# A transformer block on one core: subtractions and a mask moved from GpSimd to VectorE, and a square-root table issued later

## The chip, the core and the metric

The kernel runs on one core of a Trainium2 chip. The core has engines that work side by side, each through its own list of instructions in order: PE multiplies matrices, DVE, ACT and POOL work on vectors, and SP issues transfers. An instruction waits where its list has come to until what it needs is there, and everything behind it on the same engine waits with it. The metric is the time of one execution on the device, in microseconds (us).

## The reference, cut to what matters

One layer of a diffusion backbone: 512 latent tokens and 256 context tokens of width 1024. Normalization and modulation, one projection of all tokens by `w_in`, four groups of token mixers on its columns, an output projection, and then a mixture of 16 experts. The part in which the change lies:

```python
(na_q, na_k, na_v, dn_qkv, dn_a, dn_b, dn_gate, df_q, df_k, df_v, ft_u) = split_proj(h_lat @ w_in)
...
lower = jnp.where(strict, jnp.einsum('bnhid,bnhjd->bnhij', kb, kc) * decay, 0.0)
t_inv = lax.linalg.triangular_solve(eye + lower, ..., left_side=True, lower=True, unit_diagonal=True)
u = t_inv @ (vc * bc[..., None])
w = t_inv @ (kb * jnp.exp(gc)[..., None])
...
gate, idx = lax.top_k(jnp.swapaxes(aff, 1, 2), cap)
hid = jax.nn.silu(jnp.einsum('becd,edf->becf', xg, w_gate)) * jnp.einsum('becd,edf->becf', xg, w_up)
y = jnp.einsum('becf,efd->becd', hid, w_down) * gate[..., None]
```

The systems `eye + lower` are 64 x 64, one for each chunk, head and direction (two directions, 12 chunks of 64 tokens, 4 heads).

## The kernel before, in words

**The projection.** `w_in` is taken in 22 column blocks of 128. For each, `win` loads the raw weights `wr` by SP, and `win_parts` splits them: ACT copies them into `wh`, a type of lower precision that PE multiplies fast, and POOL makes the low part `wl = raw - wh` (line 255). The input `h` is split alike in `modulate` into `hh` (ACT) and `hl = h - hh`, for even k on DVE and for odd k on POOL (line 339). `proj_ct` then sums three products on PE: wh by hh, wl by hh, wh by hl. `wr`, `wh` and `wl` have two buffers each, so a block's parts are made while PE multiplies the block before, and the next raw load waits for its buffer.

**The order.** A scheduler gives each engine its list. It mixes the column blocks that have no place on the long path (gate, u, the neighbourhood group's q, k, v, the third group's q, k, v) in between the steps of the delta group, whose chain is: five-tap convolution (`acc`, on DVE), transposes, norms (`rs_...`), gates (`gsc`, a chain of small DVE operations that ends in `gg`), decay (`gm`, `bm` by POOL, then DVE), and the triangular systems `LT` (shown in rows as LTQ).

**The triangular systems.** The 16 x 16 blocks on the diagonal of each system are sent through DRAM (`scr`) into `Bt`, one block to a partition, and inverted there by substitution: 15 steps of `tmpb = Bt*TB` and `TB += tmpb` for two directions on DVE. `TB` and `Bt` go back through DRAM (`scr2`) into `TVc`, POOL spreads that into `TV`, and PE multiplies it by `LT`. Only the blocks off the diagonal of LT are wanted in that product. A mask `offd` clears the others; POOL does that after the blocks have been read (lines 603 to 605). `inverse` and `step` then run the recurrence over the chunks. `nql` and `nkl`, which DVE makes, are the low parts of the neighbourhood group's q and k; `dff` belongs to a block of the third group; `oacc` is the delta group's output, which `head_norm` scales.

**After it.** Attention of the other groups and the output projection, whose order on DVE and ACT is pinned, then the experts, whose weights are streamed by SP from the moment the mixers' memory is free. The last expert's output is summed into `XL`, squared on ACT for the final norm, scaled by a reciprocal square root that uses ACT's Sqrt, and stored. Functions of ACT come in tables; a change of table shows as ACT_TABLE_LOAD. One Sqrt of a constant (`small<-iota`) is issued early so that the table is there.

Of the kernel before, what the change touches and what calls it, by code (L numbers as in the profile page):

```python
# [7 lines left out]
F32 = mybir.dt.float32  # L8
I32 = mybir.dt.int32
F32R = mybir.dt.float32r  # L10
AF = mybir.ActivationFunctionType
ALU = mybir.AluOpType
# [27 lines left out]
def bc(ap, shape):  # L40
    return ap.to_broadcast(shape)


def build(tc, I, out):
    nc = tc.nc
    G, SY = nc.gpsimd, nc.sync
# [16 lines left out]
    PE, V, A = (Pinned(e) for e in (nc.tensor, nc.vector, nc.scalar))  # L63
# [3 lines left out]
    def tl(pool, shape, tag, dt=F32):  # L67
        uid[0] += 1
        return pool.tile(shape, dt, name=f"{tag}_{uid[0]}", tag=tag)
# [25 lines left out]
    with contextlib.ExitStack() as es:  # L95
# [18 lines left out]
        def pde():  # L114
            return next(alt)()

        def pb():
            uid[0] += 1
            return ps.tile([128, 1024], F32, name=f"pb_{uid[0]}", tag="pb", bufs=2)

        def load(pool, name, shape, q=None):
            t = tl(pool, shape, name)
            (q or SY).dma_start(t, I[name])
            return t

        def rhalf(c):
            return slice(c * 64, c * 64 + 64)
# [25 lines left out]
        def stg(shape, nm, dt=F32):  # L153

            uid[0] += 1
            return mp.tile(shape, dt, name=f"{nm}_{uid[0]}", tag="mx", bufs=4)
# [11 lines left out]
        def w4(which, shape, nm, dt=F32):  # L168
            uid[0] += 1
            return w4p.tile(shape, dt, name=f"{nm}_{uid[0]}", tag=f"w{which}")  # L170
# [10 lines left out]
        hh = lambda k: hh6[:, k] if k < 6 else hh2[:, k - 6]  # L181
        hl2 = [x12([128, 4, T], "hl", F32R) for _ in range(2)]
        hl = lambda k: hl2[k // 4][:, k % 4]
# [67 lines left out]
        def win_parts(raw):  # L251
            wh = w4("B", list(raw.shape), "wh", F32R)
            wl = w4("C", list(raw.shape), "wl", F32R)
            A.activation(wh, raw, AF.Copy)
            G.tensor_tensor(wl, raw, wh.bitcast(F32), op=ALU.subtract)  # L255
            return wh, wl

        def win(g, m, kh=None):
            return win_parts(win_raw(g, m, kh))
# [13 lines left out]
        with tc.tile_pool(name="st", bufs=1) as st:  # L273
# [3 lines left out]
            hT = tl(st, [128, 8, T], "hT")  # L277
# [53 lines left out]
            def modulate(q):  # L331
                kq = slice(4 * q, 4 * q + 4)
                V.scalar_tensor_tensor(a1[:, kq], mcol[:, 8 + 4 * q:12 + 4 * q, :], 1.0, bc(g1[:, kq].unsqueeze(2), [128, 4, 2]), op0=ALU.add, op1=ALU.mult)
                for k in range(4 * q, 4 * q + 4):
                    for ts, c in ((LAT, 0), (CTX, 1)):
                        A.activation(hh(k)[:, ts], hT[:, k, ts], AF.Identity, bias=mcol[:, k, c:c + 1], scale=a1[:, k, c:c + 1])
                    V.tensor_scalar(hT[:, k, L:T], hT[:, k, L:T], a1[:, k, 0:1], mcol[:, k, 0:1], op0=ALU.mult, op1=ALU.add)
                    V.tensor_scalar(hT[:, k, 0:L], hT[:, k, 0:L], a1[:, k, 1:2], mcol[:, k, 1:2], op0=ALU.mult, op1=ALU.add)
                    (G if k % 2 else V).tensor_tensor(hl(k), hT[:, k], hh(k).bitcast(F32), op=ALU.subtract)  # L339

            def first_half(b):

                w = win_parts(raws[b])
                p = pa() if b < 2 else pb()
                half.append((p[:, 0:512], p[:, 512:768] if b >= 2 else None))
                proj_ct(w, LAT, half[b][0], 0)
                if b >= 2:
                    proj_ct(w, CTX, half[b][1], 0)
# [3 lines left out]
            mod(0)  # L352
            mod(2)
            modulate(0)
            first_half(0)
            mod(1)
            first_half(1)
            m3 = mod(3)
            modulate(1)
            with tc.issue_after(m3):  # L360
                first_half(2)
# [17 lines left out]
        def b4(i, shape, nm, dt=F32):  # L379
            uid[0] += 1  # L380
            return cva.tile(shape, dt, name=f"{nm}_{uid[0]}", tag=f"b4{i}", bufs=1)
# [10 lines left out]
        for b in range(6):  # L392
            w = win(3 + b // 2, b % 2, 1 if b < 4 else None)
            raw = stg([128, NX], "raw")
# [24 lines left out]
        for kk in range(2):  # L419
            for c0, c1 in ((0, 512), (512, T)):  # L420
                for x, ht in enumerate((hh, hl)):
                    for g in range(4):
                        k = kk * 4 + g
# [95 lines left out]
        offd = load(con2, "offd", [128, 2, 64])  # L519
        blkm = load(con2, "blkm", [128, 4])  # L520
        A2 = big("C", "A2", [128, 4, 2, 8, 64])
        LT = LTQ[:, 0:3072].rearrange("p (d n h i) -> p d n h i", d=2, n=6, h=4)
# [42 lines left out]
        for c in range(2):  # L565
            for b in range(4):
                p0 = c * 64 + b * 16
                SY.dma_start(scr[c, :, :, b].rearrange("d u r i -> r (d u) i"),
                             LT[p0:p0 + 16].rearrange("p d n h i -> p (d n h) i")[:, :, b * 16:b * 16 + 16])
        Bt = b4(0, [128, 1024], "Bt")  # L570
        Bk = Bt[0:96, 0:1024].rearrange("p (c d i r) -> p d c i r", d=2, c=2, i=16)
        tmpb = b4(1, [128, 512], "tmpb")[0:96].rearrange("p (d c e) -> p d c e", d=2, c=2)
# [6 lines left out]
        for j in range(15):  # L579

            n, m = 15 - j, j + 1
# [17 lines left out]
        for q in range(2):  # L599
            for c in range(2):  # L600
                SY.dma_start(TVc[rhalf(c), q].rearrange("p d u r -> p (d u) r"), scr2[q, c].rearrange("d u b i r -> (b i) (d u) r"))

        for d in range(2):
            v = LT[:, d].rearrange("p n h i -> p (n h) i")
            G.tensor_tensor(v, v, bc(offd[:, d:d + 1, :], [128, 24, 64]), op=ALU.mult)


        A1t = {}

# [993 lines left out]
        iota = load(sm, "iota", [128, CAP])  # L1603
# [34 lines left out]
        for ee in range(last + 1):  # L1638
            pgt, pup = pb(), pb()
# [18 lines left out]
            if not ee:  # L1658
                hid, hT2 = (w4("B", [128, 1024], nm) for nm in ("hid", "hT2"))
# [3 lines left out]
                OT = w4("C", [128, 512], "OT", F32R)  # L1663
            for n in range(2):
                ns = slice(n * 512, n * 512 + 512)
                A.activation(hid[:, ns], pgt[:, ns], AF.Silu)
                V.tensor_tensor(hid[:, ns], hid[:, ns], pup[:, ns], op=ALU.mult)

            po = pde()
# [8 lines left out]
            for n in range(2):  # L1678
                pt = pa()
                for j in range(4):  # L1680
                    g, k = divmod(4 * n + j, KD)
# [36 lines left out]
            pga, small, share = pde(), w4("C", [128, 3, 4], "small"), tl(sm, [128, 1], "share")  # L1718
# [3 lines left out]
            V.tensor_copy(share, pga[:, 0:1])  # L1722
            gfin = w4("A", [128, D], "gfin")
            SY.dma_start(gfin[0:1], I["gfin"].unsqueeze(0))
            A.activation(small[:, 0, 0:1], iota[:, 0:1], AF.Sqrt)

            def scales(i0, i1):

# [165 lines left out]
```

## Time and profile before

| | |
|---|---|
| median of 3 runs | 1484.89 us (1484.33 to 1486.93) |
| profiled execution | 1486.06 us, span 1484.2 us |
| PE busy | 1329.8 us, 90% of the span |
| DVE busy | 452.4 us, 30% |
| ACT busy | 321.9 us, 22% |
| POOL busy | 237.9 us, 16% |
| mean rate from HBM | 324 GB/s |

The span is what the profile covers, from the first to the last instruction. A row of the profile names an engine, a line of the kernel and an operation as out<-in. DVE, ACT and PE instructions pass through a wrapper, so nearly all of them carry line 59; they are told apart by the tiles they write. Busy time is an average over stages with different limits, so the shares by themselves don't say what a change to one engine is worth.

### The profile page before, as it was taken

The page shows a single profiled execution, that of the slowest core. Times are in us where ns is not written, and L with a number is a line of the kernel's source. Part 1 is how long each engine was busy: PE and PEld are TensorE (multiplying, and loading weights), DVE is VectorE, ACT ScalarE, POOL GpSimd, SP SyncE. Part 2 cuts the span into 40 slices and gives each one's busy share as a digit, 9 for nine tenths or more (in the row PEclk, how much of TensorE's full clock was granted, in tenths as well). Part 3 has the DMA queues.
Part 4 walks back from the last instruction along what each step waited for, and adds up shares of the span by engine and source line. Part 5 has one row for each costly group of instructions (what it writes and reads, how often), then busy time and mean ns, then how long its engine had stood idle before and what let it go on. Part 6 is the DMA issues. An engine that isn't in the chain of part 4 may idle for free.

```text
span 1484.2 us, 20090 instructions
## 1 busy us (share of the span) xinstructions
PE 1329.8 (90%) x8422; PEld 708.6 (48%) x8422; DVE 452.4 (30%) x958; ACT 321.9 (22%) x675; POOL 237.9 (16%) x229
## 2 busy tenths in 40 slices
PE   5998969989899979999899999999999899899886
PEld 3665757776567754343343343343343343243244
DVE  4666643344573560121221211211201201112112
ACT  5424316624575211010010010010010010000113
POOL 2425727532166110000000000000000000000002
PEclk9999989999999989999999999999999999999998
DMA  9341450456684867999999999999999999999995
GB/s 355 118 144 55 107 139 17 144 178 167 231 239 157 340 283 327 427 425 428 426 427 427 427 425 428 426 427 427 427 427 425 429 425 427 427 427 426 427 402 188
DMA packets 86013, 481.56 MB, mean 324 GB/s; under 512 B 31265, under 2 KB 40097, under 8 KB 60834
## 3 DMA queue, kind: packets, MB, share of 16 engines
q1 hardware_dynamic: 85922, 480.27, 81.0%
q8 instruction: 66, 1.08, 0.3%
q14 instruction: 25, 0.20, 0.0%
HBM read 468.84 MB, written 11.40 MB: 324 GB/s over the span
## 4 chain that ended last, share of the span: by engine, by line
PE 61%; DMA 13%; DVE 9%; ACT 4%; issue 3%; POOL 1%; SPq 1%; ACTq 0%; DVEq 0%; POOLq 0%
PE pb L59 33%; PE pa L59 19%; DMA w<-in_wdown 8%; PE pd L59 5%; PE pe L59 5%; DMA w<-in_wup 3%; DMA wm<-in_wmod 2%; ACT A L59 1%; DVE XL L59 1%; DVE RT L59 1%; DVE hid L59 1%; DVE tmpb L59 1%; DVE yhl L59 1%; ACT hid L59 1%; ACT yhl L59 1%
## 5 line engine op out<-in xcount | busy, mean ns | idle before, releaser
L59 PE MATMUL pb<-w,xg 128*64 128x512 f32 x2032 | 458.3, 601 | 2.2 <-DMA w<-in_wup 1.3
L59 PEld LDWEIGHTS pb<-w,xg 128*64 128x64 f32 x2032 | 147.5, 138 | 274.9 <-issue 263.0
L59 PE MATMUL pa<-w,hT 128*64 128x512 f32 (+2 forms) x1152 | 234.4, 550 | 7.6 <-DMA w<-in_wdown 5.6
L1764 POOL TENSOR_TENSOR xo<-XL,gfin 128x384 f32<-128x384 f32 (+1 forms) x12 | 10.5, 909 | 929.7 <-DMA w<-in_wdown 923.7
L59 PEld LDWEIGHTS pa<-w,hT 128*64 128x64 f32 x1152 | 81.9, 138 | 144.8 <-issue 126.9
L59 DVE TENSOR_TENSOR hid<-hid,pb 128x512 f32<-128x512 f32 x32 | 20.6, 684 | 338.0 <-PE pb L59 338.0
L59 PE MATMUL pa<-hh,wh 128*128 128x512 f32 (+1 forms) x240 | 89.9, 388 | 7.1 <-DVE dff L59 4.3
L59 PE MATMUL pa<-hh,wl 128*128 128x512 f32 (+1 forms) x240 | 86.9, 375 | 1.3 <-POOL wl L255 1.3
L59 ACT ACTIVATE hid<-pb 128x512 f32<-128x512 f32 x32 | 17.4, 596 | 271.2 <-PE pb L59 271.2
L59 PEld LDWEIGHTS pb<-OH,xn 128*128 128x128 f32 x512 | 63.5, 200 | 25.1 <-ACT hid L59 12.4
L59 PE MATMUL pb<-OH,xn 128*128 128x128 f32 x512 | 67.7, 290 | 8.2 <-ACT hid L59 7.1
L59 DVE TENSOR_TENSOR hid<-pa,XL 128x512 f32<-128x512 f32 x15 | 10.4, 692 | 208.0 <-PE pa L59 208.0
L59 DVE SCALAR_TENSOR_TENSOR XL<-pe,aff,XL 128x512 f32<-128x512 f32 x60 | 44.8, 747 | 76.2 <-PE pd L59 70.2
L59 PE MATMUL pe<-yhl,OT 64*128 64x512 f32 x120 | 47.4, 458 | 17.7 <-ACT yhl L59 10.2
L255 POOL TENSOR_TENSOR wl<-wr,wh 128x1024 fp32r<-128x1024 f32 (+1 forms) x22 | 50.9, 2315 | 74.6 <-ACT wh L59 71.9
L59 PE MATMUL pd<-yhl,OT 64*128 64x512 f32 x120 | 47.4, 458 | 15.9 <-ACT yhl L59 8.7
L59 DVE SCALAR_TENSOR_TENSOR XL<-pd,aff,XL 128x512 f32<-128x512 f32 x60 | 44.8, 746 | 50.4 <-PE pe L59 46.4
L59 PEld LDWEIGHTS pa<-hh,wh 128*128 128x128 f32 x240 | 47.5, 198 | 23.4 <-issue 5.2
L59 PE MATMUL pa<-hl,wh 128*128 128x512 f32 (+1 forms) x240 | 55.0, 361 | 0.9 <-POOL hl L339 0.9
L59 ACT ACTIVATE yhl<-hid 128x512 fp32r<-128x512 f32 x15 | 9.5, 631 | 203.9 <-DVE hid L59 189.0
L59 PEld LDWEIGHTS pa<-hh,wl 128*128 128x128 f32 x240 | 47.4, 198 | 9.2 <-POOL wl L255 2.3
L59 PEld LDWEIGHTS pa<-hl,wh 128*128 128x128 f32 x240 | 39.6, 188 | 8.6 <-POOL hl L339 1.3
(387 smaller groups left out, 1640.8 us busy)
## 6 DMA issues: line engine op xcount, KB each, us to landing
w<-in_wgate SPq DMA_DIRECT2D x64, 2048.0 KB, 34.0
w<-in_wup SPq DMA_DIRECT2D x63, 2048.0 KB, 35.4
w<-in_wdown SPq DMA_DIRECT2D x60, 2048.0 KB, 35.9
wm<-in_wmod SPq DMA_DIRECT2D x32, 512.0 KB, 7.2
wr<-in_win SPq DMA_DIRECT2D x18, 512.0 KB, 3.4
wm<-in_wmod SPq DMA_DIRECT2D x8, 1024.0 KB, 12.1
w<-in_wdown SPq DMA_DIRECT2D x8, 768.0 KB, 12.6
wr<-in_wout SPq DMA_DIRECT2D x16, 256.0 KB, 5.8
```

The costliest lines, as they stand in the source:

```text
L59: r = f(*args, **kw)
L255: G.tensor_tensor(wl, raw, wh.bitcast(F32), op=ALU.subtract)
L1764: G.tensor_tensor(xo[i][:, cols], xl[:, i, cols], gfin[:, cols], op=ALU.mult)
```

## The change

Three things go from POOL to DVE: the 26 subtractions that make `wl`, the four `hl` of odd k, and the mask on LT. The mask is also written further ahead, in front of the code of the substitution. Fourth, the Sqrt of a constant near the end is issued after the last Silu.

```diff
             A.activation(wh, raw, AF.Copy)
-            G.tensor_tensor(wl, raw, wh.bitcast(F32), op=ALU.subtract)
+            V.tensor_tensor(wl, raw, wh.bitcast(F32), op=ALU.subtract)
             return wh, wl
...
-                    (G if k % 2 else V).tensor_tensor(hl(k), hT[:, k], hh(k).bitcast(F32), op=ALU.subtract)
+                    V.tensor_tensor(hl(k), hT[:, k], hh(k).bitcast(F32), op=ALU.subtract)
...
+        for d in range(2):
+            v = LT[:, d].rearrange("p n h i -> p (n h) i")
+            V.tensor_tensor(v, v, bc(offd[:, d:d + 1, :], [128, 24, 64]), op=ALU.mult)
         Bt = b4(0, [128, 1024], "Bt")
...
-        for d in range(2):
-            v = LT[:, d].rearrange("p n h i -> p (n h) i")
-            G.tensor_tensor(v, v, bc(offd[:, d:d + 1, :], [128, 24, 64]), op=ALU.mult)
...
-                A.activation(hid[:, ns], pgt[:, ns], AF.Silu)
+                silu = A.activation(hid[:, ns], pgt[:, ns], AF.Silu)
...
-            A.activation(small[:, 0, 0:1], iota[:, 0:1], AF.Sqrt)
+            with tc.issue_after(silu.ins):
+                A.activation(small[:, 0, 0:1], iota[:, 0:1], AF.Sqrt)
```

The scheduler then makes new lists, and more moves than the edits say. Three places of the lists follow. The first is DVE's list just ahead of the substitution; the names end in the number of their buffer. Before:

```order
L59 TENSOR_TENSOR nql_2668<-pa_2642,nqh_2667 128x512
L59 SCALAR_TENSOR_TENSOR nkl_2730<-pa_2679,nkh_2729 128x512
L59 SCALAR_TENSOR_TENSOR nkl_2730<-pa_2704,nkh_2729 128x256
L59 TENSOR_SCALAR Bt_1243<-Bt_1243 96x1024
L59 TENSOR_TENSOR tmpb_1244<-Bt_1243,TB_1246 96x2x15 x2
```

The same place on DVE in the changed kernel:

```order
L59 TENSOR_TENSOR wl_2740<-wr_2737,wh_2739 128x1024
L59 SCALAR_TENSOR_TENSOR nkl_2730<-pa_2679,nkh_2729 128x512
L59 SCALAR_TENSOR_TENSOR nkl_2730<-pa_2704,nkh_2729 128x256
L59 TENSOR_TENSOR wl_2803<-wr_2800,wh_2802 128x1024
L59 TENSOR_TENSOR LTQ_876<-LTQ_876,offd_1045 128x1536 x2
L59 TENSOR_TENSOR wl_2860<-wr_2857,wh_2859 128x1024
L59 TENSOR_SCALAR Bt_1245<-Bt_1245 96x1024
L59 TENSOR_TENSOR tmpb_1246<-Bt_1245,TB_1248 96x2x15 x2
```

Three wl and the two halves of the mask now stand ahead of Bt, the first instruction of the substitution; wl_2860, for the second k block of the neighbourhood group, is the last of them.

The second place is DVE's list in `head_norm`, where the copy of a third-group block (dff_3128) stands among the small operations of the norm. Before:

```order
L59 SCALAR_TENSOR_TENSOR rs_z1h_528_3514<-rs_ah_527_3511,rs_z0h_526_3509 128x16
L59 TENSOR_TENSOR rs_ah_529_3516<-rs_z1h_528_3514 128x16
L59 TENSOR_TENSOR rs_ah_529_3516<-rs_ah_529_3516,rs_th_522_3499 128x16
L59 SCALAR_TENSOR_TENSOR rs_z2h_530_3519<-rs_ah_529_3516,rs_z1h_528_3514 128x16
L59 TENSOR_TENSOR oacc_1322<-oacc_1322,rs_z2h_530_3519 128x256
L59 COPY dff_3128<-pa_3103 128x256
```

In the changed kernel:

```order
L59 TENSOR_TENSOR rs_ah_525_3506<-rs_ah_525_3506,rs_th_522_3499 128x16
L59 COPY dff_3128<-pa_3103 128x256
L59 SCALAR_TENSOR_TENSOR rs_z0h_526_3509<-rs_ah_525_3506,rs_jh_524_3503 128x16
L59 TENSOR_TENSOR rs_ah_527_3511<-rs_z0h_526_3509 128x16
L59 TENSOR_TENSOR rs_ah_527_3511<-rs_ah_527_3511,rs_th_522_3499 128x16
L59 TENSOR_TENSOR si_3043<-pa_3135,si_3043 128x512
L59 TENSOR_TENSOR wl_3213<-wr_3210,wh_3212 128x1024
```

The copy is now in front of rs_z0h instead of behind the first oacc.

The third place is the end of ACT's list, from the last expert's one-hot tile (OT) to its hidden units (hid), as a piece of the difference:

```order
+L59 ACTIVATE OT_5443<-pe_8496 128x512
+L59 ACTIVATE hid_5440<-pb_8378 128x512 x2
 L59 ACT_TABLE_LOAD
 L59 ACTIVATE small_8524<-iota_5300 128x1
-L59 ACTIVATE OT_5443<-pe_8496 128x512
-L59 ACT_TABLE_LOAD
-L59 ACTIVATE hid_5440<-pb_8378 128x512 x2
 L59 ACTIVATE gfin_8535<-pe_8578 128x512
```

One table load now stands behind the two Silu, and a later one, behind the last square and ahead of the last small, is gone from the list.

Elsewhere: in the gsc chain of DVE one wl (wl_2605) stands six places ahead of gg, and another behind gg. On POOL the first TV follows directly on operations of the recurrence, where a wl stood ahead of it. On PE the transposes of the convolved keys (pd_881 and on), which begin the chain of norms and gates, stand earlier, ahead of projection matmuls of the gate's second block. On ACT the gate's second Silu stands behind the Exp of the gates instead of ahead of it, with a table load on each side. From the output projection on, the lists of PE and SP and the pinned ones are the same, but for the end.

## Rows read from the trace of the kernel before

**Rows 1.** Windows: each engine's busy time (instructions), PE clock, DMA share, GB/s.

```profile
549.00:1441.00 892.00, 824.53 (x4137) 332.06 (x4137) 142.50 (x220) 71.51 (x129) 0.00 (x0) 0.99 0.99 419
```

**Rows 2.** PE's waits, 40 to 349 us: total us, times, longest.

```profile
PE pa L59 <- DVE nql L59: 9.2, 1, 9.2
PE pe L59 <- DVE gsc L59: 4.8, 1, 4.8
PE pa L59 <- DVE dff L59: 4.3, 1, 4.3
PE pd L59 <- POOL gm L537: 2.3, 3, 0.9
...
PE pb L59 <- POOL TV L619: 1.7, 1, 1.7
...
PE pa L59 <- POOL wl L255: 1.3, 2, 0.8
PE pa L59 <- POOL hl L339: 0.9, 1, 0.9
```

**Rows 3.** Timeline of DVE, 126 to 136 us: start, us, instruction.

```profile
127.97 2.37 DVE L59 TENSOR_TENSOR rs_a<-rs_a,rs_t 128x48 f32<-128x48 f32 x1
...
130.86 0.20 DVE L59 TENSOR_TENSOR rs_a<-rs_a,rs_t 128x48 f32<-128x48 f32 x1
...
134.41 2.38 DVE L59 TENSOR_SCALAR gsc<-gsc 128x48 f32<-128x48 f32 x1
```

**Rows 4.** Timeline of POOL, the same stretch; in brackets the idle time before.

```profile
134.10 2.65 POOL L255 TENSOR_TENSOR wl<-wr,wh 128x1024 fp32r<-128x1024 f32 x1 [3.83 <-ACT wh L59]
```

**Rows 5.** Timeline of DVE, the substitution.

```profile
178.02 1.44 DVE L59 TENSOR_SCALAR Bt<-Bt 96x1024 f32<-96x1024 f32 x1 [5.51 <-DMA Bt<-scr]
179.50 5.71 DVE L59 TENSOR_TENSOR tmpb<-Bt,TB 96x30 f32<-96x30 f32 x2
...
188.54 2.58 DVE L59 TENSOR_TENSOR TB<-TB,tmpb 96x120 f32<-96x120 f32 x2
...
191.52 0.47 DVE L59 TENSOR_TENSOR TB<-TB,tmpb 96x126 f32<-96x126 f32 x2
```

**Rows 6.** Timeline of POOL, from the mask to the first TV.

```profile
175.42 7.40 POOL L605 TENSOR_TENSOR LTQ<-LTQ,offd 128x1536 f32<-128x1536 f32 x2
...
210.04 2.36 POOL L255 TENSOR_TENSOR wl<-wr,wh 128x1024 fp32r<-128x1024 f32 x1 [19.26 <-ACT wh L59]
212.37 2.33 POOL L619 TENSOR_TENSOR TV<-TVc,blkm 128x256 f32<-128x256 f32 x4
```

**Rows 7.** Timelines of DVE and POOL, 301 to 305 us.

```profile
301.62 2.51 DVE L59 TENSOR_TENSOR oacc<-oacc,rs_z2h 128x256 f32<-128x256 f32 x1
304.06 0.41 DVE L59 COPY dff<-pa 128x256 f32<-128x256 f32 x1
...
301.51 2.34 POOL L255 TENSOR_TENSOR wl<-wr,wh 128x1024 fp32r<-128x1024 f32 x1
```

**Rows 8.** POOL's groups by form: xcount, busy us, mean ns, idle before.

```profile
L255 POOL TENSOR_TENSOR wl<-wr,wh 128x1024 fp32r<-128x1024 f32 x18 | 45.2, 2511 | 71.3 <-ACT wh L59 68.7 <-issue 2.6
```

**Rows 9.** DVE's groups by form, 40 to 349 us.

```profile
L59 DVE TENSOR_TENSOR nql<-pa,nqh 128x512 fp32r<-128x512 f32 x2 | 1.4, 682 | 1.1 <-ACT nqh L59 1.1
```

**Rows 10.** Windows, PE alone: length, busy (instructions), granted clock, DMA share, GB/s.

```profile
132.00:138.00 6.00, 6.00 (x49) 0.62 0.37 126
160.00:180.00 20.00, 19.97 (x111) 1.00 0.72 182
304.50:310.50 6.00, 5.98 (x14) 0.50 0.45 109
```

**Rows 11.** Timeline of ACT, after a block of the neighbourhood group.

```profile
181.34 1.09 ACT L59 ACTIVATE wh<-wr 128x1024 fp32r<-128x1024 f32 x1
```

**Rows 12.** Timeline of ACT, the end.

```profile
1445.74 0.60 ACT L59 ACTIVATE gfin<-pe 128x512 f32<-128x512 f32 x1 [4.91 <-PE pe L59]
...
1472.85 1.28 ACT L59 ACT_TABLE_LOAD   x1
1474.14 0.30 ACT L59 ACTIVATE small<-small 128x1 f32<-128x1 f32 x2
```

## The prediction

> **What bounds the kernel now.** I read the 40 slices and the windows first, then PE's waits, then the timelines of DVE, POOL and ACT at those waits, and the end last. From 549 to 1441 us the reader is to see a stage of transfers: 419 GB/s and a DMA share of 0.99, no POOL work at all, little DVE work [rows 1]. Nothing that this change moves can shorten it. But its first loads wait for memory that the mixer stages free, so a front that ends earlier moves the whole of it forward. What matters are the first 349 us and the last 43.
>
> In the front PE runs its list in order, and its waits are few and long [rows 2]: 9.2 us for DVE's nql, 4.8 for DVE's gsc, 4.3 for DVE's dff, 2.3 for POOL's gm, 1.7 for POOL's TV, 1.3 for POOL's wl, 0.9 for POOL's hl. Only the last two are waits for what the change moves. The three longest are for DVE, which gets more work. So the question is why DVE was late there.
>
> **DVE is late because POOL holds it.** Next to each other, the timelines of both engines show it. A 128x48 rs_a takes 0.20 us, but 2.37 when it starts at 127.97; a 128x48 gsc took 2.38 at 134.41 [rows 3]. At 134.10 a wl had begun on POOL, for 2.65 us [rows 4], and the gsc ends when it does (136.8); under the rs_a lies the wl before it. The substitution shows the same: tmpb x2 takes 5.71 us and TB x2 2.58, where a larger TB x2 takes 0.47 [rows 5], and POOL's mask (7.40 us for its two halves, from 175.42) and further wl lie over them [rows 6]. So does the third: oacc 2.51 us, with dff queued behind it, while a wl runs on POOL [rows 7].
> The Trainium skill ("SBUF — State Buffer", Who interferes with whom) says that GpSimd and VectorE share a pair of ports, that a VectorE instruction with two SBUF inputs or in a two-port mode contends with a GpSimd one that reads SBUF, and that the second to issue is blocked until the first is done. The rows agree: the ends coincide. The rule also speaks against the change, since each moved subtraction has two SBUF inputs and can itself be held by what stays on POOL; that is in the first rival.
>
> **The change, part by part.** POOL loses 18 wl of 128x1024 at 2.51 us [rows 8], the smaller wl, four hl and the mask. DVE gets them. Its price isn't shown for 128x1024; a subtraction of 128x512 took 0.68 there [rows 9], so a 1024 is bounded by 0.68 and 1.38, and I take 1.38. DVE is busy for 30% of the span, so the sum is no bound; what counts is where they stand.
>
> First, PE's direct waits before 80 us: 0.9 + 1.3 = 2.2. The same copy on ACT precedes them, and then 1.4 us replaces up to 2.9. DVE is dense there; I take 2.0 (0 to 2.2).
>
> Second, the gsc chain. The two holds go: 2.37 - 0.20 + 2.38 - 0.20 = 4.35. One wl now stands among its last instructions: 1.38. The chain is 3.0 shorter, and of PE's 4.8 us, 1.8 would be left. The transposes that begin the chain also stand ahead of projection matmuls that were ahead of them, which PE can now do while it waits; so I take all 4.8. The clock adds to it. It was 0.62 of full speed in 132 to 138, the 6 us after that gap, in which PE worked without a pause [rows 10]: (1 - 0.62) x 6.0 = 2.3 us. Without the gap that goes too. Together 7.1 (from -1.4, if the inserted wl only adds, to 7.1). POOL's gm (2.3) stays where it is: 0 (0 to 2.3, if POOL starts them sooner).
>
> Third, the substitution. It starts when Bt lands, at 178.02 [rows 5]. It loses holds of (5.71 - 0.47) + (2.58 - 0.47) = 7.3 us. But ahead of it in DVE's list now stands wl_2860. That needs ACT's wh, which in the row of before began at 181.34 for 1.09, behind the copies nvcT and nvT of a projection [rows 11]. On DVE it would end at 181.34 + 1.09 + 1.38 = 183.8, 5.8 us after Bt has landed. PE was busy in all of 160 to 180 [rows 10], so that projection and the triangular systems move forward about alike and the 5.8 stays. Gain: 7.3 - 5.8 = 1.5 (0 to 7.3, if the wait doesn't bind). Queued behind it are the whole substitution and nql, for which PE waits. The mask costs nothing on DVE: it waits only until the transfers out of LT have read it, and Bt's own transfer comes after those; if that cover went, it would be at most the 7.4 of POOL's two.
>
> Fourth, POOL's TV. It is behind a wl at 210.04, itself late on ACT's wh by 19.26 [rows 6]; PE waits 1.7 for it. POOL's list has no wl there now: 1.7 (0 to 1.7).
>
> Fifth, the recurrence to 295. Two or three wl land between its X's on DVE. PE has little idle time there, so I charge 0.5 (0 to 3 x 1.38 = 4.1).
>
> Sixth, the blocks after 295. dff's copy waited behind oacc [rows 7], PE 4.3 us for it. In the new list it stands eight instructions earlier, behind instructions of 0.2 us: perhaps 0.5 is left, gain 3.8. The clock after the gap was 0.50 for 6.0 us [rows 10]: 3.0 more. Together 6.8 (0 to 6.8).
>
> Seventh, the end. ACT loads a table at 1472.85 for 1.28 us, on the path to the output [rows 12]. With the Sqrt issued behind the last Silu, the table is loaded once, in ACT's 4.91 us of idle time before gfin, and stays: 1.3 (0 to 1.3).
> The Trainium skill ("ScalarE: Activation LUTs", What ACT_TABLE_LOAD costs) puts a switch at 1283 ns for the load and 1380 ns more for a drain, 2.66 in all; the trace agrees with the load alone, since small begins 1.29 us after it. By the page this term would be 2.7; the sum goes by the row.
>
> Two more table loads stand in the front of the new ACT list, one ahead of the late gate's Silu and one ahead of eg. I cost them at nothing, as ACT waits there for PE; uncovered they cost 1.28 each.
>
> Sum: 2.0 + 7.1 + 1.5 + 1.7 - 0.5 + 6.8 + 1.3 = 19.9 us. The profiled execution took 1486.06 (span 1484.2): 1466.2. The median of the runs is 1.2 lower than it: 1465.0.
>
> **The rivals.** (A) DVE's own order takes most of it back. Each wl is in DVE's list at a fixed place and waits there for ACT's copy; in the gsc chain that, or a hold by what POOL still does, keeps gg as late as before. (The Trainium skill's page above has such holds; no row shows one of a wl.) Then the second term is 0, the third 0, the fifth -2: 2.0 + 1.7 - 2.0 + 6.8 + 1.3 - some 2 of clock that stays = about 8, 1477. For it: nql's wait shows what one late instruction costs. Against: the copies are mostly done early. (B) The holds have another cause, and only direct waits go: 2.2 + 1.7 + 1.3 = 5.2 less the moved work on the path, some 3: 1482.7. Against it: the ends coincide in three places. (C) The wait at wl_2860 doesn't bind, because ACT gets to its copy sooner: the third term is 7.3: 1465.0 - 5.8 = 1459.2. (D) The front ends earlier, but 349 to 549 waits for its own loads, and only the end is won: 1483.5. Against it: those loads are issued when memory is freed, by the same front. (E) Slower: wl_2860 is very late, and with it everything on DVE. Each us beyond 183.8 is lost to PE; 1.5 is eaten at 185.3, and the rest of the sum, 18.4, at 203.7. From there on the kernel is slower; at 210, where a wl of before did stand because of ACT, by 6.3 us: 1491. What speaks against it is that nothing between 182 and 203 is known to hold ACT [rows 11].
>
> **How the numbers follow.** Forecast as summed 0.52, (A) 0.18, (C) 0.16, (B) 0.05, (D) 0.05, (E) 0.04. The time is that of the forecast, 1465.0. The range reaches past (C) by gm's 2.3 and some 2 more of clock (no row bounds the clock after a shorter gap), and past (A) by 1: 1455 to 1478; what is left out is (B), (D) and (E), 0.14, and some of the edges. A measurement of this kernel tells about 0.2%, 3 us, from no change. Faster: forecast, (A), (C) and most of (B), 0.92. Same: (D) and the rest of (B), 0.05. Slower: 0.03.
>
> **What would show it.** Right, if gsc and rs_a take about 0.2 us throughout, tmpb and TB under 0.6, oacc 0.41; if PE's waits for gsc and dff fall under 1 us, that for TV is gone, and that for nql is about 7.5; if wl_2860 ends some 6 us after Bt lands; if the stream of weights starts 18 to 19 us earlier; if no table load follows the last Square. Wrong, if DVE's small instructions stay long although POOL is idle (B), if DVE waits for wh for more than 6 us anywhere ahead of the substitution (A, E), if the wait at wl_2860 is under 2 us (C), or if the stream starts as late as before (D).

## The result, and the profile after

| | before | changed |
|---|---|---|
| median (4 runs each, taken together) | 1485.83 us (1484.33 to 1486.93) | 1464.84 us (1462.40 to 1467.22) |
| ratio of the runs | | 0.986, 95% interval 0.9845 to 0.9875 |
| profiled execution, span | 1486.06, 1484.2 us | 1462.40, 1460.6 us |
| DVE, POOL busy | 452.4, 237.9 us | 450.5, 170.1 us |

The forecast was 1465.0 us, in a range of 1455 to 1478. DVE took over 32 instructions and is busy 2 us less than before: the time for which POOL no longer holds it is about as long as the work that it took over. Later comparisons use another profiled execution of the changed kernel too (called the second one; its median there was 1464.94), since single executions differ by up to 5 us.

The first view is PE's waits from 40 to 340 us, with the total, the number and the longest. It answers to [rows 2].

```profile
PE pa L59 <- DVE nql L59: 6.5, 1, 6.5
PE pe L59 <- DVE gsc L59: 2.6, 1, 2.6
PE pd L59 <- POOL gm L537: 2.3, 3, 0.9
...
PE pa L59 <- DVE dff L59: 1.8, 1, 1.8
```

POOL's wl, hl and TV are gone from the list; the three long waits for DVE are shorter, and none of them is gone. The second view is DVE's timeline in the gsc chain, the counterpart of [rows 3], and POOL's beside it.

```profile
118.11 0.85 DVE L59 TENSOR_TENSOR rs_a<-rs_z 128x48 f32<-128x48 f32 x1
118.89 1.08 DVE L59 TENSOR_TENSOR gsc<-gsc 128x48 f32<-128x48 f32 x1
119.89 0.20 DVE L59 TENSOR_TENSOR rs_a<-rs_a,rs_t 128x48 f32<-128x48 f32 x1
...
125.58 1.22 DVE L59 TENSOR_TENSOR wl<-wr,wh 128x1024 fp32r<-128x1024 f32 x1
126.72 0.18 DVE L59 TENSOR_SCALAR gsc<-gsc 128x48 f32<-128x48 f32 x1
...
117.85 2.05 POOL L538 TENSOR_TENSOR bm<-minc,be 128x512 f32<-128x512 f32 x2 [2.76 <-DVE rs_z L59]
```

The two instructions of 2.4 us are at 0.20 and 0.18; the wl among them costs 1.22. Two are still long, 0.85 and 1.08, and both lie under POOL's two bm, which stayed there; in the kernel before they stood there too (0.86 at 126.19 and 1.08 at 126.97). The third view is the way into the substitution, on ACT and then on DVE ([rows 5] and [rows 11]).

```profile
170.92 0.38 ACT L59 ACTIVATE nvcT<-pa 128x256 f32<-128x256 f32 x1 [7.00 <-PE pa L59]
171.20 1.21 ACT L59 ACTIVATE nvT<-pa 128x256 f32<-128x256 f32 x4
172.26 1.09 ACT L59 ACTIVATE wh<-wr 128x1024 fp32r<-128x1024 f32 x1
```

```profile
165.09 3.42 DVE L59 TENSOR_TENSOR LTQ<-LTQ,offd 128x1536 f32<-128x1536 f32 x2
173.38 1.23 DVE L59 TENSOR_TENSOR wl<-wr,wh 128x1024 fp32r<-128x1024 f32 x1 [4.87 <-ACT wh L59]
174.53 0.68 DVE L59 TENSOR_SCALAR Bt<-Bt 96x1024 f32<-96x1024 f32 x1
175.24 0.30 DVE L59 TENSOR_TENSOR tmpb<-Bt,TB 96x30 f32<-96x30 f32 x2
...
185.48 0.68 DVE L59 TENSOR_TENSOR nql<-pa,nqh 128x512 fp32r<-128x512 f32 x1
```

No row of the substitution is long any more: it takes 11 us, from 174.53 to nql at 185.48, where it took 19.2. But it starts behind the wl that waited 4.87 us for ACT, as forecast.

How far each event of the front moved, from the timelines of PE and SP in both profiled executions:

| event | before | changed | earlier by |
|---|---|---|---|
| first transposes of the normed keys (the wait for gsc) | 132.00 | 121.73 | 10.3 |
| PE goes on behind nql | 197.97 | 186.22 | 11.8 |
| first product of TV and LT | 213.03 | 201.18 | 11.9 |
| PE goes on behind dff | 304.52 | 289.28 | 15.2 |
| first transposes of the block after it | 322.20 | 304.13 | 18.1 |
| first load of the experts' weights | 488.11 | 467.18 | 20.9 |
| last Silu | 1439.74 | 1418.79 | 21.0 |
| end of the span | 1484.2 | 1460.6 | 23.6 |

From the first load of weights to the last Silu it is 951.6 us in both, so the front's gain goes through whole. The last three rows hold noise: the second profiled execution of the changed kernel has its transposes at 304.23, as here, but its first load at 470.66 and its end at 1463.9.

### The profile page after: what moved, and what is told of

It reads as the page before. It is cut to its first block, busy times and chain, and to the rows that moved or that the text cites. A ratio compares the mean times of both kernels' runs of the same rounds, so it can differ in the third digit from the quotient of the medians.

```text
span 1460.6 us, 20081 instructions
## 1 busy us (share of the span) xinstructions
PE 1321.5 (90%) x8422; PEld 705.4 (48%) x8422; DVE 450.5 (31%) x990; ACT 321.2 (22%) x675; POOL 170.1 (12%) x197
## 3 DMA queue, kind: packets, MB, share of 16 engines
q8 instruction: 66, 1.08, 0.3%
## 4 chain that ended last, share of the span: by engine, by line
PE 68%; DMA 16%; DVE 8%; ACT 5%; issue 1%; POOL 1%; SPq 1%; ACTq 0%; DVEq 0%; POOLq 0%
PE pb L59 34%; PE pa L59 24%; DMA w<-in_wdown 8%; PE pd L59 6%; PE pe L59 5%; DMA w<-in_wup 3%; DMA w<-in_wgate 3%; DMA wm<-in_wmod 2%; ACT A L59 1%; DVE XL L59 1%; DVE RT L59 1%; DVE hid L59 1%; ACT hid L59 1%; DVE yhl L59 1%; ACT yhl L59 0%
## 5 line engine op out<-in xcount | busy, mean ns | idle before, releaser
L1764 POOL TENSOR_TENSOR xo<-XL,gfin 128x384 f32<-128x384 f32 (+1 forms) x12 | 10.6, 915 | 928.1 <-DVE XL L59 928.1
L59 PE MATMUL pa<-hh,wh 128*128 128x512 f32 (+1 forms) x240 | 86.7, 375 | 4.4 <-ACT hh L59 1.9
L59 DVE TENSOR_TENSOR hid<-pa,XL 128x512 f32<-128x512 f32 x15 | 10.4, 692 | 206.3 <-PE pa L59 206.3
L59 PE MATMUL pe<-yhl,OT 64*128 64x512 f32 x120 | 47.2, 456 | 17.6 <-ACT yhl L59 10.2
L59 PEld LDWEIGHTS pe<-yhl,OT 64*128 64x128 f32 x120 | 18.6, 184 | 46.2 <-ACT yhl L59 16.4
## 6 DMA issues: line engine op xcount, KB each, us to landing
wm<-in_wmod SPq DMA_DIRECT2D x8, 1024.0 KB, 11.5
```

The costliest lines, as they stand in the source:

```text
L59: r = f(*args, **kw)
L1764: G.tensor_tensor(xo[i][:, cols], xl[:, i, cols], gfin[:, cols], op=ALU.mult)
```

## The experiments

All times are medians in us, each of at least four runs; each of four sets of runs had its own runs of the kernel before on the same chip (1483.7, 1484.28, 1485.4, 1485.91), and the ratio is to those.

**The changed kernel again,** as a base. No edit.

> The changed kernel once more, as the base for the three others on this chip: 1464.8 us give or take 2.5, which is how far its four earlier runs lay apart. PE waits 6.5 us for nql again and starts the first product of TV and LT at about 201 us.

1464.94, ratio 0.987 (0.9851 to 0.9889); waits and event as expected (200.96). The main experiments compare with this one.

**Does POOL hold DVE, and by what?** The lists of PE, DVE and ACT stay; only POOL gets work in the substitution, whose result nobody uses. Once it reads:

```diff
         V.tensor_scalar(Bt[0:96, 0:1024], Bt[0:96, 0:1024], -1.0, None, op0=ALU.mult)
+        idle = tl(con2, [128, 512], "idle")
+        for _ in range(6):
+            G.tensor_tensor(idle[0:96], Bt[0:96, 0:512], Bt[0:96, 512:1024], op=ALU.mult)
```

> Six products of two halves of Bt, 96x512 each, run on POOL during the substitution, into a tile that nobody reads; the lists of PE, DVE and ACT are the same as in the changed kernel. If POOL's reading of SBUF holds DVE's two-input instructions: each product (about 1.0 us) lets one DVE instruction pass at its end, tmpb and TB rows of 1 to 2 us appear, the substitution of 10.9 us takes 5 to 6 us more, PE's wait for nql goes from 6.5 to about 12, and the time rises by 5 to 6 us. If the long DVE rows of before had another cause: the substitution stays at 10.9 us and the time within 1 us.

And once it only writes:

```diff
+        idle = tl(con2, [128, 1024], "idle")
+        G.tensor_scalar(idle[0:96, 0:32], Bt[0:96, 0:32], 1.0, None, op0=ALU.mult)
+        for _ in range(6):
+            G.memset(idle[0:96], 0.0)
```

> As the run before, but POOL only writes: one small copy of 96x32 out of Bt, then six memsets of 96x1024. If it is POOL's reading that holds DVE's two-input instructions: no long rows but one of a few tenths under the copy, time within 1 us of the changed kernel. If any work on POOL holds DVE: again 4 to 6 us more.

Timelines of POOL and DVE with the reads:

```profile
175.86 8.10 POOL L585 TENSOR_TENSOR idle<-Bt 96x512 f32<-96x512 f32 x6 [20.42 <-DVE Bt L59]
...
175.99 1.37 DVE L59 TENSOR_TENSOR TB<-TB,tmpb 96x30 f32<-96x30 f32 x2
177.31 1.48 DVE L59 TENSOR_TENSOR tmpb<-Bt,TB 96x56 f32<-96x56 f32 x2
178.71 1.39 DVE L59 TENSOR_TENSOR TB<-TB,tmpb 96x56 f32<-96x56 f32 x2
```

And with the writes:

```profile
176.77 5.98 POOL L586 MEMSET idle<- 96x1024 f32 x6
...
176.50 0.30 DVE L59 TENSOR_TENSOR TB<-TB,tmpb 96x30 f32<-96x30 f32 x2
176.74 0.38 DVE L59 TENSOR_TENSOR tmpb<-Bt,TB 96x56 f32<-96x56 f32 x2
177.03 0.34 DVE L59 TENSOR_TENSOR TB<-TB,tmpb 96x56 f32<-96x56 f32 x2
```

With POOL reading, the same DVE rows are four times as long, and PE's wait for nql goes from 6.5 to 12.9: 6.4, where 5 to 6 was expected. The time was 1473.07, ratio 0.9933 (0.9908 to 0.9957), 8.1 above the base; 6.2 to 6.6 of that stand in the front of the trace, the rest lies within what executions differ by. With POOL writing for 6 us, no row changed, PE waits 6.6, and the time was 1463.98 (0.9873; 0.9847 to 0.9899), that of the base. So it is reading by POOL, not its being busy, that holds DVE's two-input instructions. The page "SBUF — State Buffer" of the Trainium skill (Who interferes with whom) draws that line, and both runs agree with it. That settles rival (B) against. One held row of before is of another kind: the gsc of 2.38 us at 134.41 has one input only. These two runs have no such instruction, so for that one only the ends that coincide speak.

**Which of the edits carries the gain?** wl back on POOL, the rest as changed:

```diff
-            V.tensor_tensor(wl, raw, wh.bitcast(F32), op=ALU.subtract)
+            G.tensor_tensor(wl, raw, wh.bitcast(F32), op=ALU.subtract)
```

> The changed kernel with wl back on POOL: hl, the mask and the Sqrt stay as changed. If wl is what holds DVE and delays PE, most of the gain goes: what is left is 0.9 us of hl, about 3 in the substitution (the mask's hold is gone, those of two wl come back) and 1.3 to 2.6 at the end, so 5 to 7 us under the kernel before; gsc, oacc and TB rows of 2.3 to 2.6 us are there again and PE waits 4 to 5 us for gsc and for dff. If the mask and hl did most of it: within 5 us of the changed kernel.

1480.84 (ten runs), ratio 0.997 (0.9958 to 0.9983): 3.4 under the kernel before, somewhat less than the 5 to 7. Its waits (PE, 100 to 310) are those of before but for nql, which is where the mask was:

```profile
PE pa L59 <- DVE nql L59: 5.7, 1, 5.7
PE pe L59 <- DVE gsc L59: 4.8, 1, 4.8
PE pa L59 <- DVE dff L59: 4.3, 1, 4.3
...
PE pb L59 <- POOL TV L618: 1.7, 1, 1.7
```

The opposite, the kernel before with wl alone on DVE:

> The kernel before with nothing changed but wl, which goes to DVE; hl of odd k, the mask and the Sqrt stay. If wl alone carries the gain, as its return to POOL says: the first 0.9 us of hl's wait comes back and little else (the mask lies under the wait for wl_2860, the Sqrt gained nothing), so 1466 to 1468 us. If the four edits need each other: 1470 or more.

1468.89, ratio 0.9892 (0.9858 to 0.9925): 17 under its kernel before, against 21 for all four edits, and 1 above what was expected. PE waits 1.6 for wl at the start there, 0.4 in the changed kernel. wl is some four fifths of the change. The first event of the table comes at 126.22 us with wl alone, at 132.22 with hl but not wl, at 121.73 with both and at 132.00 with neither: without wl, hl gains nothing there, and beside it some 4.5. The end is 1.1 longer than in the changed kernel, since the Sqrt stands at its old place (more on this below). None of these runs parts the holds from the new order of the lists, which wl brings with it: dff's copy went ahead of oacc by the order.

The mask back on POOL, at its old place:

```diff
-        for d in range(2):
-            v = LT[:, d].rearrange("p n h i -> p (n h) i")
-            V.tensor_tensor(v, v, bc(offd[:, d:d + 1, :], [128, 24, 64]), op=ALU.mult)
         Bt = b4(0, [128, 1024], "Bt")
...
+        for d in range(2):
+            v = LT[:, d].rearrange("p n h i -> p (n h) i")
+            G.tensor_tensor(v, v, bc(offd[:, d:d + 1, :], [128, 24, 64]), op=ALU.mult)
```

> The changed kernel with the mask back on POOL at its old place; the other lists are the same. POOL starts it when the transfers out of LT have read it, at about 165 us, and is done at about 172.5, before the substitution starts behind wl_2860 at about 174. So although the mask held the substitution of before by some 5 us, it should hold nothing here: time within 1 us of the changed kernel, substitution 10.9 us. If the move of the mask is worth something by itself: 3 to 5 us more than the changed kernel.

POOL's and DVE's timelines ahead of the substitution:

```profile
163.19 7.96 POOL L605 TENSOR_TENSOR LTQ<-LTQ,offd 128x1536 f32<-128x1536 f32 x2 [6.99 <-DMA scr<-LTQ]
...
165.23 2.55 DVE L59 TENSOR_TENSOR wl<-wr,wh 128x1024 fp32r<-128x1024 f32 x1 [0.52 <-ACT wh L59]
174.67 1.23 DVE L59 TENSOR_TENSOR wl<-wr,wh 128x1024 fp32r<-128x1024 f32 x1 [6.88 <-ACT wh L59]
175.81 0.68 DVE L59 TENSOR_SCALAR Bt<-Bt 96x1024 f32<-96x1024 f32 x1
```

The mask on POOL is over at 171.2 and holds one wl (2.55 instead of 1.23), for which nothing waits; PE's wait for nql is 6.5 again. The median was 1467.75 with runs from 1460.56 to 1468.52 (0.9873; 0.9843 to 0.9902): 2.8 above the base, but the ratio is the base's, and the events of the front are late by 1.5 from the first (123.0 for 121.5) to the last (305.7 for 304.2), so nothing is lost between them. So the move of the mask by itself shows nothing, because of the wait for wl_2860; in the kernel before the mask did hold the substitution.

**What is the wait at wl_2860 worth?** That one wl goes behind the substitution:

```diff
-            V.tensor_tensor(wl, raw, wh.bitcast(F32), op=ALU.subtract)
+            with tc.issue_after(late) if late is not None else contextlib.nullcontext():
+                V.tensor_tensor(wl, raw, wh.bitcast(F32), op=ALU.subtract)
...
-            return win_parts(win_raw(g, m, kh))
+            return win_parts(win_raw(g, m, kh), sub[0].ins if (g, m) == (1, 1) else None)
...
-                V.tensor_tensor(dst, dst, t, op=ALU.add)
+                sub = [V.tensor_tensor(dst, dst, t, op=ALU.add)]
```

> The wl of the second k block (wl_2860) is issued behind the substitution instead of ahead of it; nothing else is edited, though the lists behind that place move a little. If the wait for it costs what the trace says (the substitution starts 6 us after Bt has landed): the substitution starts at about 168.6 us, PE's wait for nql falls from 6.5 to about 1, the slow clock behind that wait goes too, and the time falls by 6 to 8 us, to about 1458. If another wait takes its place (PE waits for this wl itself, or for TV, since fewer projections are left to cover the way of TB through memory): 0 to 3 us less.

DVE's timeline at the start of the substitution, and PE's where it goes on behind nql:

```profile
170.21 0.69 DVE L59 TENSOR_SCALAR Bt<-Bt 96x1024 f32<-96x1024 f32 x1 [0.48 <-DMA Bt<-scr]
...
182.00 1.12 PE L59 MATMUL pa<-ident,nvT 128*128 128x128 f32 x4 [1.10 <-DVE nql L59]
184.00 0.79 PE L59 MATMUL pa<-hh,wl 128*128 128x512 f32 x1 [0.45 <-DVE wl L59]
```

The substitution starts with Bt's landing and PE's wait falls to 1.1, as expected. The slow clock behind the wait didn't go, as this window shows; in the six us behind the wait of the base (186.01 to 192.01) it was 0.66:

```profile
182.00:188.00 6.00, 5.54 (x14) 0.50 0.78 233
```

The first product of TV and LT came at 196.55, 4.4 earlier, although this execution was 1.5 late before. But the time was 1462.20, ratio 0.9851 (0.9831 to 0.9871): 2.7 under the base, not 6 to 8. From that product to the wait for dff it takes 2.0 longer, 90.4 for 88.4. The windows of PE over just these two stretches, the second execution of the changed kernel first, show why:

```profile
200.96:289.38 88.42, 82.33 (x1699) 1.00 0.38 110
```

```profile
196.55:286.98 90.43, 85.07 (x1708) 1.00 0.35 111
```

The new list does nine matmuls of projections more there, and PE is busy 2.7 us longer: less was done before the product. Of the 4.4 at the event 2.0 were borrowed. The first theory's place was right and its size was not.

**The table at the end.** The Sqrt issued where it was:

```diff
-            with tc.issue_after(silu.ins):
-                A.activation(small[:, 0, 0:1], iota[:, 0:1], AF.Sqrt)
+            A.activation(small[:, 0, 0:1], iota[:, 0:1], AF.Sqrt)
```

> The changed kernel with the Sqrt of a constant issued where it was: three table loads at the end again, the last of them on the path. By the row of before (1.28 us) the stretch from the last Silu to the end is 1.3 us longer, by the Trainium skill's page on ScalarE (load and drain) 2.7; the front is the same to 1 us.

1466.26, ratio 0.9883 (0.986 to 0.991): 1.3 above the base, less than medians can tell. ACT's timeline at the end tells more. The changed kernel first, then this one:

```profile
1450.20 0.19 ACT L59 ACTIVATION_READ_ACCUMULATOR hid<-XL 128x1 f32 x1
...
1453.00 2.19 ACT L59 ACTIVATE xo<-xo,small 128x1024 f32<-128x1024 f32 x2 [1.48 <-DVE small L59]
```

```profile
1450.58 0.19 ACT L59 ACTIVATION_READ_ACCUMULATOR hid<-XL 128x1 f32 x1
1450.79 1.28 ACT L59 ACT_TABLE_LOAD   x1
1452.08 0.30 ACT L59 ACTIVATE small<-small 128x1 f32<-128x1 f32 x2
1453.26 2.19 ACT L59 ACTIVATE xo<-xo,small 128x1024 f32<-128x1024 f32 x2 [0.89 <-DVE small L59]
```

ACT's xo comes no earlier without the load: it starts 2.80 us behind the last sum of squares, and 2.68 with the load. ACT waits for DVE instead, whose own xo stands ahead of three small operations that ACT's xo needs. But DVE's xo is a part of the output too, and that part is early. DVE, and SP with the stores, in the changed kernel:

```profile
1451.68 0.75 DVE L59 TENSOR_SCALAR xo<-xo,small 128x1024 f32<-128x1024 f32 x1
1452.35 0.16 DVE L59 TENSOR_TENSOR small<-small 128x3 f32<-128x3 f32 x1
...
1452.46 3.08 SPq L1773 DMA_DIRECT2D out<-xo  x4
```

And in this run:

```profile
1453.16 1.42 DVE L59 TENSOR_SCALAR xo<-xo,small 128x1024 f32<-128x1024 f32 x2
1453.94 2.91 SPq L1772 DMA_DIRECT2D out<-xo  x4
```

Counted from the last sum of squares, DVE's first xo starts at 1.48 us instead of 2.58, the first store is issued at 2.26 instead of 3.36, and the span ends at 10.4 instead of 11.5. The other traces agree: 10.2 to 10.5 in all eight with the later Sqrt and this order of xo, 11.5 to 11.6 in the three with the Sqrt at its old place (the kernel before, this run, wl alone). So the later Sqrt is worth 1.1 us at the end, through DVE's share of the output.

The next run goes by the stretch to ACT's xo alone: DVE's xo is issued behind the small operations.

```diff
-                    V.tensor_scalar(xo[i], xo[i], r3[i], None, op0=ALU.mult)
+                    with tc.issue_after(last.ins):
+                        V.tensor_scalar(xo[i], xo[i], r3[i], None, op0=ALU.mult)
```

> The changed kernel with DVE's two xo issued behind the last of the small operations on which ACT's xo waits; nothing else differs. In the changed kernel the stretch from the last Square's sum to ACT's xo is 2.80 us although the table load is gone (2.69 before). If DVE's xo of 0.75, which stands ahead of three small operations, took the load's place: the stretch is about 2.0 us, 0.7 to 0.9 less, and the whole time less by as much, which single runs can't show. If something else holds the small operations: it stays at 2.8.

```profile
1455.77 1.41 DVE L59 TENSOR_SCALAR xo<-xo,small 128x1024 f32<-128x1024 f32 x2
1456.55 2.89 SPq L1775 DMA_DIRECT2D out<-xo  x4
```

The stretch to ACT's xo is 1453.73 to 1455.95, 2.22: 0.6 shorter, near what was expected. But DVE's first xo starts 0.56 later than in the changed kernel (2.04 behind the last sum for 1.48), the first store with it, and from that sum to the end of the span it takes 11.0 us, for 10.4. So this order takes half of the Sqrt's gain back, and the stretch to ACT's xo was the wrong measure. The time, 1465.50 (0.9864; 0.9845 to 0.9884), can't show either.

**Further.** bm on DVE too, on top of wl_2860 behind the substitution:

```diff
-            G.tensor_tensor(bm, mk, bc(be[:, :, p, :].unsqueeze(3), [128, 2, 4, 64]), op=ALU.mult)
+            V.tensor_tensor(bm, mk, bc(be[:, :, p, :].unsqueeze(3), [128, 2, 4, 64]), op=ALU.mult)
```

> The kernel with wl_2860 behind the substitution, and bm (six products of 128x512 that POOL makes ahead of each gm) moved to DVE as well. If POOL's bm holds DVE in the norm chain and delays POOL's own gm: the rs_a and gsc rows of 0.85 and 1.08 go, but two bm of 0.7 stand there instead, so PE's wait for gsc stays near 2.6; the gm rows of 1.42 on DVE become 0.7, PE's waits for POOL's gm (2.3) fall under 1, and the time falls by 1 to 3 us. If DVE's list is now what the chain waits for: 0 to 3 us more.

1460.94, ratio 0.9837 (0.9815 to 0.9859). PE's wait for gsc fell to 1.1, which was not expected, and that for gm stayed at 2.2, which was not either. The wait for nql was replaced by one as long, as the timelines of PE and ACT show:

```profile
182.99 1.97 PE L59 MATMUL pa<-ident,nvT 128*128 128x128 f32 x8 [6.04 <-ACT nvc L59]
...
181.61 1.06 ACT L59 ACTIVATE wh<-wr 128x1024 fp32r<-128x1024 f32 x1 [3.02 <-DMA wr<-in_win]
182.57 0.37 ACT L59 ACTIVATE nvc<-pa 128x256 f32<-128x256 f32 x1
```

ACT's nvc is now behind a wh that waits for its raw weights. With wl_2860 behind the substitution and DVE's xo behind the small operations, without and with bm on DVE:

> Both orders mended: wl_2860 behind the substitution, and xo behind the small operations. If the two gains add: 2.7 + 0.8 under the changed kernel, about 1461.4, and clear of the kernel before by 22 to 24 us.

> The same with bm on DVE too: about 1460.2 if all three gains add (1460.9 was measured without the xo order).

1459.89 (1459.83 to 1461.23), ratio 0.9833 (0.9818 to 0.9847), and 1463.04, ratio 0.9852 (0.9835 to 0.987). So bm on DVE is not shown to be worth anything. The two orders together have the lowest median: 25.5 under their kernel before, and 5 under the changed kernel, all of whose runs lie above theirs. By ratios they can't be told from wl_2860 behind the substitution alone (0.9851), and the order of xo has no part in it: from the last sum of squares to the end it takes 10.7 us there, for 10.2 with wl_2860 alone.

## Why the prediction was right, point by point

The mechanism (reading by POOL holds DVE, and PE waits for DVE) was shown by the pair of runs that read and wrote. The sum of 19.9 met the 21.0 of the medians, but some of its terms were off and cancelled, which is luck.

- First term, direct waits: 2.0 forecast. hl's wait is gone and wl's is 0.4: 2.2 became 0.4, so 1.8.
- Second, the gsc chain: this step failed in its working. It set both holds (4.35) against the inserted wl (1.38), and then took all 4.8 of the wait, and the clock with it. But PE's wait ended at 132.00, with transposes of kn, as the prediction's own window of the clock from 132 says. The row of before, then that of the changed kernel:

```profile
132.00 0.66 PE L59 MATMUL pe<-ident,kn 128*128 128x128 f32 x2 [4.81 <-DVE gsc L59]
```

```profile
121.73 0.41 PE L59 MATMUL pe<-ident,kn 128*128 128x128 f32 x2 [2.62 <-DVE gsc L59]
```

  The hold at 134.41 comes behind the end of the wait, and so does the inserted wl (125.58): neither is a part of it. Only the hold at 127.97 lies ahead: 2.37 - 0.20 = 2.17 off 4.81 leaves 2.64, and 2.62 was measured. The holds under bm are in what is left, so the sign of 0.2 us throughout had to fail, and that of a wait under 1 us with it. The clock behind the wait was still low:

```profile
122.00:126.00 4.00, 4.00 (x42) 0.57 0.02 4
```

  That is 4.0 x 0.43 = 1.7 us lost for 2.3 before, so wait and clock gave 2.2 + 0.6 = 2.8, not 7.1. Yet the event is 10.3 earlier. Up to it PE was idle 5.1 us less, by all waits together, and did 574 matmuls instead of 585: eleven of 128x512, some 0.23 us each, stand behind it now, which is 2.5 of the gain. The other 2.6 is busy time of the same matmuls and stays open. The words on the transposes were right about the move, but not about what it does: it didn't fill the wait, it put the event ahead.
- Third, the substitution: 1.5 forecast; the event behind nql moved from 10.3 to 11.8, 1.5. That they agree is partly luck: the eleven matmuls are done in this stretch, and PE is idle 3.1 less in it. At its end both kernels have done the same projections, so the 11.8 is gain in full, where the first three terms made 10.6. wl went to DVE at 1.26 us each (18 of 128x1024) where 1.38 was taken.
- Fourth, TV: 1.7 forecast, 0.1 found at the event. The wait is gone, and six matmuls of a projection, some 1.4 us, that stood behind the product are done in its place (PE is busy 14.96 us in that stretch for 13.35).
- Fifth and sixth, to the wait for dff: -0.5 + 3.8 = 3.3 forecast, 3.4 found. Here too the agreement is partly luck: those six matmuls are 1.4 of it. PE's wait fell by 2.5 only, to 1.8 (under 1 had been a sign of being right), because a small operation ahead of dff's copy was held once more by a POOL product that stayed (DVE at 287.61: 1.28 us for 0.17; POOL's dff at 287.60: 1.26). That leaves some -0.5 for the recurrence, as charged. The clock behind the gap: 3.0 forecast, and from dff to the next transposes 17.7 became 14.9, 2.8, all at full clock:

```profile
289.28:304.13 14.85, 14.85 (x75) 1.00 0.50 170
```

- Seventh, the end: 1.3 forecast, 1.1 found, but not by the way that was forecast: ACT's xo is no earlier, DVE's is. The Trainium skill ("ScalarE: Activation LUTs", What ACT_TABLE_LOAD costs), with its drain of 1380 ns, would have had 2.7; in the run with the old order, small follows 1.29 us after the start of the load, as before, so no drain is seen there.

To the transposes behind dff the front gained 18.1 where 18.6 had been forecast, and the end 1.1. The other 2 us of the medians are not assigned: in single executions of kernels with the same lists there, the stretch from those transposes to the first load of weights was 163.0 to 166.4 us, and that from the last Silu to the last sum of squares 31.4 to 33.3, while before's one profile has 165.9 and 32.9. In the front, from 32 us on, PE was idle 11.4 us less and busy 6.7 less; the slow clock explains some 3 of the latter by the rows. The rest stays open, and may lie in the modelled ends of matmuls.

Of the rivals, (A) was there in small (the wait at wl_2860, which the sum had priced); (B) was refuted by the runs that read and wrote, (D) by 951.6 us on both sides; (C) and (E) did not occur: wl_2860 waited 4.87.

## What to carry to other kernels

An engine that PE waits for may be late because of a second one that no wait names: lay the timelines of both side by side, and look for rows of one form with two durations, the longer of which ends with the other engine's instruction. Moving work onto the engine that is waited for can then make it faster. Charge a hold to a wait only if it lies ahead of that wait's end. An event that comes earlier proves no gain as long as the lists ahead of it differ: count the instructions and the busy time up to it, and compare where the lists are the same again. And when a load or a wait is taken off the end, measure to the last store: an instruction that comes no earlier may share the output with one that does.

## What was not expected of the hardware

- Six POOL memsets of 96x1024, 6 us in all, left DVE's two-input instructions at their usual 0.30 to 0.38 us; six POOL products of 96x512 made them 1.4.
- The hold goes both ways: those six products took 8.10 us, 1.35 each, where POOL's 128x512 product bm took 1.03 each beside short DVE work (2.05 for two), and the mask on POOL took 7.96 with a wl on DVE beside it, for 7.40 in [rows 6]; that wl took 2.55 for 1.23.
- After a pause of 2.6 us PE worked at a mean granted clock of 0.57 for the next 4 us (a mean over its two levels, 1.2 and 2.4 GHz); after one of 1.8 us (the wait for dff) it stayed at 1.00. After two pauses of 1.7 and 1.1 us with four short matmuls between them it was 0.50 for 6 us (182 to 188, wl_2860 behind the substitution).
